# A nanmax over 65536 rows on one Trainium2 core: one tile's write-backs counted on their engines' own semaphores

## The chip, the cores and the metric

The kernel runs on one core of one Trainium2 chip. The metric is the device time of one execution in microseconds. Three engines do the arithmetic: VectorE (DVE in the profile), ScalarE (ACT) and GpSimd (POOL). SyncE (SP) only issues the DMA transfers. TensorE is not used.

## The reference

```python
def setup_inputs():
    batch, seq, dim = 32, 2048, 2048
    x = np.random.randn(batch, seq, dim).astype(np.float32)
    mask = np.random.rand(batch, seq, dim) < 0.1
    x[mask] = np.nan
    return {"x": x, "axis": -1}

def reference(x, axis):
    return np.nanmax(x, axis=axis).astype(np.float32)
```

For each of 65536 rows of 2048 floats, a tenth of them NaN, the largest value that is not NaN. The input is 537 MB; the output is 65536 floats.

## The kernel before, in words

**The work on one element.** VectorE's reduction with `max` needs the NaNs out of the way first, and that takes two passes over the upper 16 bits of each float, both in place in the tile. In the first, ScalarE makes a *key* (line 271, `kt<-xt`): it reads the upper halves of a tile `xt` and writes 16-bit keys into a key buffer `kt`. In the second, the *write-back*, the keys are turned back into upper halves in `xt`, with the NaNs now very low numbers. Most write-backs are done by GpSimd (line 281, `xt<-kt`), some small ones by ScalarE itself (line 271 too, `xt<-kt`). Then VectorE reduces whole rows to their maxima (line 288).

**Tiles.** A tile is 128 partitions by 28 quarters of a row (a quarter is 512 columns, so a full tile is 14336 columns, 7 rows in each partition). There are 74 tiles in 6 groups; three tile buffers, `xt0` to `xt2`, are used in turn, tile 64 being in `xt0`. Maxima of the first groups go to `acc`, those of tiles 61 to 74 to `lead`, which is how the profile tells them apart. The list `TILES` gives for each tile, in quarters: how it is loaded, in which pieces it is keyed and written back, and which maxima are taken. In the pieces a negative number is a piece that ScalarE writes back, a positive one a piece of GpSimd; a float (`-4.0`) tells that ScalarE's write-back is issued behind the next key. The tiles around the change are

```python
    + [([16, 12], [-4.0, 12, 12], [4, 12, 12])]     # tile 63
    + [([17, 11], [-4.0, 12, 12], [16, 12])]        # tile 64
    + [([17, 11], [11, 6, (4, -7)], [8, 8, 12])]    # tile 65
```

Tile 64 is loaded in 17 and 11 quarters. Its first 4 quarters (2048 columns) are ScalarE's, the next 12 (6144 columns) GpSimd's, and so are the last 12. Its first maximum takes 16 quarters, that is the first two pieces at once; its second takes the last piece. Tile 63 has the same pieces, but a maximum for each of them.

**Key buffers.** Three, `kt0` to `kt2`, of 6144 columns each, used in turn. A key that opens a buffer waits until those that read the buffer's last keys, the write-backs, are done: `kfree` holds these events. In addition, the last key of a tile waits for those who read the *next* buffer's keys (lines 410 to 412), so that the next tile's first key needs no wait for them. In tiles 63 and 64 alike the three pieces go to `kt0`, `kt1` and `kt2`.

**Order and waits.** The program is written out by hand; each engine works through its instructions in order. `Order.add` (line 166) gives each instruction the waits that it needs: an event is a semaphore and a count, waits that another wait already implies are dropped (`needed`, line 150), the last one is put on the instruction, and the others stand alone in front of it. Normally an instruction counts on its engine's own semaphore (`act`, `pool`, `dve`).

**Pairs.** An instruction can be given a semaphore of its own instead. Where one maximum needs one write-back of GpSimd and one of ScalarE, and no other maximum needs either, `joints` (line 91) makes the two a pair: both count on one semaphore, `pair64_1` in tile 64, and the maximum waits for its count 2. `cleaned` (line 369) then notes that one event, count 2, as the event of both write-backs, in `kfree` too.

**Loads.** SP issues the loads in order; a load waits until the last maximum of the tile that had the buffer is done. They all go through one queue.

Of the kernel before, what the change touches and what calls it, by code (L numbers as in the profile page):

```python
# [54 lines left out]
FLAGGED = (3, 5)  # L55
LATE = 4

APART = ()
WIDE = 7
BUFS = 3  # L60

# [29 lines left out]
def joints(pieces, reds):  # L91

    flat = []
    at = 0
    for step, parts in enumerate(pieces):  # L100
        for c in parts if isinstance(parts, tuple) else (parts,):

            if with_last(c):
                flat[-1] = (flat[-1][0], at + abs(c), False, step)
            else:
                flat.append((at, at + abs(c), c < 0, step + isinstance(c, float)))
            at += abs(c)
    needs = []
    done = 0
    for n in reds:  # L110
        over = [i for i, (a, b, _, _) in enumerate(flat) if a < done + n and b > done]
        done += n
        pools = [i for i in over if not flat[i][2]]
        backs = [i for i in over if flat[i][2]]
        if pools and backs and flat[pools[-1]][3] > flat[backs[-1]][3]:
            backs = []
        needs.append(pools[-1:] + backs[-1:])
    pairs = {}
    for need in needs:
        if len(need) == 2 and all(sum(i in n for n in needs) == 1 for i in need):  # L120
            for i in need:
                pairs[i] = tuple(need)
    return pairs
# [61 lines left out]
def kernel(  # L185
# [146 lines left out]
    for gi, (s, g) in enumerate(zip(rows, GROUPS)):  # L332
# [6 lines left out]
        for loads, pieces, reds in g:  # L339
# [19 lines left out]
            pairs = {}  # L359
            if number not in APART:  # L360
                pairs = joints(pieces, [n // Q for n in reds])
# [178 lines left out]
```

## Time and profile before

| | |
|---|---|
| median of three runs | 1254.84 us (1254.7 to 1254.85) |
| the profiled execution | 1254.63 us |
| its span, first to last instruction | 1253.3 us |
| read from HBM | 536.87 MB, 429 GB/s over the span |
| reductions to `acc`, 4 rows, 8192 columns | 53 of 8.687 us |
| reductions of 3 rows, 6144 columns | 6.544 us (`acc`), 6.546 us (`lead`) |
| GpSimd write-backs of 6144 columns | 64 of 7.041 us |
| ScalarE keys of 6144 columns | 64 of 5.321 us |

All times on the profile's axis are counted from the first instruction. Line 271 holds both of ScalarE's operations; `kt<-xt` is a key and `xt<-kt` a write-back. The timeline merges neighbouring instructions of a line, gives the first start, the time from there to the last end and the number of them, and in brackets how long the engine was idle before and what ended that. The chain of waits follows back from the last instruction what each step waited for.

### The profile page before, as it was taken

How to read it: one execution, taken by the hardware profiler on the slowest of the kernel's cores; microseconds unless marked ns; L12 is line 12 of the kernel's file. 1: busy time of each engine (PE TensorE's matmuls, PEld its weight loads, DVE VectorE, ACT ScalarE, POOL GpSimd, SP SyncE). 2: the span in 40 equal slices, each digit the busy share in tenths (PEclk: the TensorE clock that was granted, in tenths of full speed). 3: DMA queues.
4: the chain of work that ended last, by engine and by line, in shares of the span. 5: the costliest groups of instructions: out<-in, count | busy, mean ns of one | idle time of the engine just before them, and what ended most of it. 6: DMA issues, size and time to landing. Idle time of an engine off the chain costs nothing.

```text
span 1253.3 us, 892 instructions
## 1 busy us (share of the span) xinstructions
DVE 1111.0 (89%) x187; ACT 968.2 (77%) x281; POOL 1165.2 (93%) x240
## 2 busy tenths in 40 slices
DVE  0888989888889988898988888898888899899999
ACT  3777887778777877788777877776777779889997
POOL 2999989998999899998999899999999999899997
DMA  9999999999999999999999999999999999999996
GB/s 414 439 421 428 439 439 440 432 417 439 439 438 436 430 425 439 439 437 436 426 428 439 439 437 434 419 437 439 437 436 430 425 439 426 436 433 428 432 425 269
DMA packets 16855, 537.20 MB, mean 429 GB/s; under 512 B 2640, under 2 KB 2640, under 8 KB 4944
## 3 DMA queue, kind: packets, MB, share of 16 engines
q1 hardware_dynamic: 16848, 537.14, 99.2%
q14 instruction: 7, 0.06, 0.0%
HBM read 536.87 MB, written 0.26 MB: 429 GB/s over the span
## 4 chain that ended last, share of the span: by engine, by line
DMA 35%; DVE 34%; POOL 19%; ACT 10%; issue 0%; SPq 0%
DMA xt<-in_x_dram 35%; DVE acc L288 22%; POOL xt L281 19%; DVE lead L288 13%; ACT kt L271 9%; ACT xt L271 1%; SPq L247 0%; DVE none L294 0%; DVE lead L308 0%; SPq L265 0%; SPq L256 0%
## 5 line engine op out<-in xcount | busy, mean ns | idle before, releaser
L281 POOL TENSOR_SCALAR xt<-kt 128x6144 int16<-128x6144 uint16 (+10 forms) x234 | 1164.1, 4975 | 80.5 <-ACT kt L271 66.6
L271 ACT ACTIVATE kt<-xt 128x3584 uint16<-128x3584 int16 (+10 forms) x249 | 912.7, 3705 | 272.7 <-DMA xt<-in_x_dram 242.2
L288 DVE TENSOR_REDUCE acc<-xt 128x3 f32<-128x6144 f32 (+4 forms) x121 | 894.8, 7435 | 133.5 <-POOL xt L281 126.2
L288 DVE TENSOR_REDUCE lead<-xt 128x1 f32<-128x2048 f32 (+4 forms) x59 | 212.4, 3682 | 3.5 <-POOL xt L281 3.5
L271 ACT ACTIVATE xt<-kt 128x512 int16<-128x512 uint16 (+4 forms) x30 | 57.1, 1912 | 0.6
L271 ACT ACT_TABLE_LOAD x1 | 1.3, 1283 | 3.3 <-PEq L265 3.3
L314 DVE MEMSET lead<- 128x1 f32 x1 | 0.1, 59 | 3.3 <-PEq L265 3.3
L288 DVE TENSOR_REDUCE xt<-xt 128x1 f32<-128x1536 f32 (+1 forms) x2 | 2.4, 1211 | 0.0
L294 DVE TENSOR_SCALAR none<-acc 128x414 int32<-128x414 f32 x1 | 0.6, 593 | 0.0
L294 POOL TENSOR_SCALAR lead<-lead 128x91 int32<-128x91 f32 x1 | 0.5, 547 | 0.1
L308 DVE TENSOR_TENSOR acc<-acc,none 128x414 int32<-128x414 int32 x1 | 0.6, 586 | 0.0
L308 POOL TENSOR_TENSOR lead<-lead 128x91 int32<-128x91 int32 x1 | 0.4, 378 | 0.1
L521 POOL MEMSET const-float32-0.0<- 128x1 f32 x1 | 0.1, 99 | 0.2 <-issue 0.2
L271 ACT ACTIVATE lead<-lead 128x1 f32<-128x1 f32 x1 | 0.2, 203 | 0.0
L294 DVE TENSOR_SCALAR none<-lead 128x7 int32<-128x7 f32 x1 | 0.2, 169 | 0.0
L308 DVE TENSOR_TENSOR lead<-lead,none 128x7 int32<-128x7 int32 x1 | 0.2, 163 | 0.0
L521 POOL MEMSET const-bfloat16-1.0<- 128x1 bf16 x1 | 0.1, 103 | 0.0
L521 POOL MEMSET const-uint8-127<- 128x1 uint8 x1 | 0.1, 102 | 0.0
L521 POOL MEMSET const-float32-1.0<- 128x1 f32 x1 | 0.1, 99 | 0.0
## 6 DMA issues: line engine op xcount, KB each, us to landing
xt<-in_x_dram SPq DMA_DIRECT2D x61, 7168.0 KB, 22.6
xt<-in_x_dram SPq DMA_DIRECT2D x3, 4096.0 KB, 16.8
xt<-in_x_dram SPq DMA_DIRECT2D x5, 2048.0 KB, 23.7
xt<-in_x_dram SPq DMA_DIRECT2D x3, 3072.0 KB, 23.6
xt<-in_x_dram SPq DMA_DIRECT2D x2, 4352.0 KB, 16.3
xt<-in_x_dram SPq DMA_DIRECT2D x3, 2816.0 KB, 23.1
xt<-in_x_dram SPq DMA_DIRECT2D x2, 3584.0 KB, 21.3
xt<-in_x_dram SPq DMA_DIRECT2D x5, 1024.0 KB, 25.1
```

Source lines behind the costliest of these rows:

```text
L271: lambda: nc.scalar.activation(**kw),
L281: lambda: nc.gpsimd.tensor_scalar(**kw),
L288: return order.add("dve", nc.vector, lambda: do(**kw), deps)
L294: lambda: engine.tensor_scalar(out=none, in0=acc, scalar1=NONE, scalar2=float(0x00800000), op0=ALU.is_equal, op1=ALU.mult,),
L308: lambda: engine.tensor_tensor(out=bits, in0=bits, in1=none, op=op),
L314: e_warm = order.add("dve", nc.vector, lambda: nc.vector.memset(warm, 1.0), [])
L521: nc = _bacc.Bacc("TRN2", target_bir_lowering=False, num_devices=1)
```

## The change

Tile 64 is put on a list of tiles that have no pairs:

```diff
-APART = ()
+APART = (64,)
```

The list is read in one place, line 360: `if number not in APART: pairs = joints(...)`. In tile 64 the write-back of ScalarE then counts on `act` and that of GpSimd on `pool`. The waits that follow from it, as `Order` writes them (everything else is the same but for the numbers of the counts):

```diff
  # VectorE: the first maximum of tile 64, 16 quarters
-   waits pair64_1
+   waits act, pool
  # ScalarE: the last key of tile 64, kt2 <- xt0, 6144 columns
-   waits pool, load9, pair64_1
+   waits pool, load9, act
  # ScalarE: the second key of tile 65, kt1 <- xt1, 3072 columns
-   waits nothing
+   waits pool
```

No instruction is added, taken away or moved on any engine, apart from the wait in front of the maximum that stands alone.

## The prediction

> **What bounds the kernel now.** I read the page first: its shares, then section 4. The shares name no single bound.
>
> ```profile
> DVE 1111.0 (89%) x187; ACT 968.2 (77%) x281; POOL 1165.2 (93%) x240
> ...
> DMA 35%; DVE 34%; POOL 19%; ACT 10%; issue 0%; SPq 0%
> ```
>
> The load queue is busy for 99.2% of the span (section 3) and GpSimd for 93%, yet the chain changes hands, so I asked for it in order of time, from tile 64 on (1072 us to the end).
>
> ```profile
> 1079.80 5.33 ACT kt L271
> 1085.13 0.07 issue
> 1085.20 7.06 POOL xt L281
> 1092.26 0.02 issue
> 1092.28 6.55 DVE lead L288
> 1098.83 0.01 issue
> 1098.84 144.79 DVE lead L288 x45
> 1243.63 0.84 issue
> 1244.47 6.68 DVE lead L288 x3
> ```
>
> From 1092.28 on the end is set by VectorE reductions alone. Just before, three steps stand one after the other: GpSimd's write-back (1072.73 to 1079.76), then a ScalarE key, then GpSimd again. The waits from 1050 us to the end say the same: VectorE waits once in all that time.
>
> ```profile
> ACT kt L271 <- POOL xt L281: 9.2, 4, 4.9
> DVE lead L288 <- POOL xt L281: 3.5, 1, 3.5
> ACT kt L271 <- DMA xt<-in_x_dram: 1.4, 2, 0.9
> ```
>
> The longest wait in line 1 (4.9) is ScalarE's at 1079.80, and the 3.5 is VectorE's at 1092.28. The timeline shows both, and tile 63 beside them:
>
> ```profile
> 1057.52 2.48 ACT L271 ACTIVATE xt<-kt 128x2048 int16<-128x2048 uint16 x1
> 1060.03 5.32 ACT L271 ACTIVATE kt<-xt 128x6144 uint16<-128x6144 int16 x1
> ...
> 1072.39 2.47 ACT L271 ACTIVATE xt<-kt 128x2048 int16<-128x2048 uint16 x1
> ...
> 1079.80 10.11 ACT L271 ACTIVATE kt<-xt 128x6144 uint16<-128x6144 int16 x2 [4.94 <-POOL xt L281]
> ```
>
> In tile 63 ScalarE goes from its write-back to the tile's last key in 0.03 us (1057.52 + 2.48 = 1060.00, then 1060.03). In tile 64, with the same pieces, it stands still for 4.94 us.
>
> **Why it waits, and what the change does there.** The last key of a tile waits also for whoever last read the key buffer that comes next (lines 410 to 412). For tile 64 the key goes to kt2 and the next buffer is kt0, which ScalarE's own small write-back (2048 columns) read. But that write-back is half of a pair (lines 369 to 381): its entry is the pair's event, count 2, and the second count is GpSimd's write-back of the other 6144 columns, out of kt1. So ScalarE waits for GpSimd over a buffer that GpSimd does not use. Tile 63 has a maximum of its own for its small piece, hence no pair, hence no such wait. With tile 64 in APART the entry becomes ScalarE's own count. Both programs have the same instructions in the same order on each engine; the waits differ in three places.
>
> **1. The last key of tile 64.** It still has three waits, two of them standing alone as before. They are due: the load of its columns, issued 1050.37, landing 21.6 later, 1072.0; GpSimd's write-back of tile 63, that frees kt2, 1065.60 + 7.05 = 1072.65; ScalarE's write-back, 1072.39 + 2.47 = 1074.86. With tile 63's 0.03 the key starts at 1074.89, not 1079.80: 4.91 earlier. Ended at 1074.89 + 5.32 = 1080.21.
>
> **2. GpSimd behind it.** It follows a key by 0.08 (1085.12 to 1085.20), so its write-back runs 1080.29 to 1087.33 in place of 1085.20 to 1092.25.
>
> **3. VectorE.** Back to back, a reduction starts 0.08 before the recorded end of the last: two of 6.54 and 8.68 make 15.14 from 1073.65, ending 1088.79. The next can start at 1088.71 instead of 1092.28: 3.57. The one after it, at 1098.84, now 0.01 behind its forerunner, wins its 0.08 of overlap as well: 3.66 in all. Its data are there: the load issued 1065.11 lands 17.2 later at 1082.3, the key takes 4.88 (1087.2), GpSimd 1087.41 to 1093.89, wanted at 1095.18. The Trainium skill (VectorE: DVE Perf Modes, The DRAIN you can't avoid) says that the next operation does not start until the pipeline has emptied. By that rule nothing of the overlap is regained and the sum would be 3.49; the trace's 15.14 speaks for 3.66.
>
> **4. The maximum's two waits.** One more standing wait on VectorE, ScalarE's count, due at 1074.86, while the reduction in front runs to 1080.20; GpSimd's count, on the instruction, is due at 1079.76 as before. Behind it are tile 64's second maximum and the load that refills xt0. A gain is excluded, since a wait is only added. The floor is 0: the last maximum of the kernel has a standing wait too, done at 1243.63 in the chain, and it lies inside reductions that run on without a gap (1240.09 to 1246.76, 6.67 for three of 2.28). The ceiling is a lost overlap and a restart, 0.08 + 0.03. I take 0, by that row, which is the same engine and the same kind of wait. If ScalarE's write-back came after 1080.1, this wait would cost what it came late.
>
> **5. A key of tile 65** (kt1, 3072 columns) now waits for GpSimd's write-back out of kt1, which the pair had covered. That ended at 1079.76 and the key can't start before 1087.1: cover 7 us, cost 0.
>
> **What is late next.** SP issues each refill when a maximum frees the buffer, so these go 3.6 earlier, but the load engines have no idle time to win: their share is 1.00 from 1092 to 1190, and the last load lands at 1243.15 either way. So I held VectorE's starts, moved by 3.66, against the write-backs with loads kept where they are. Two narrow places:
> - The third write-back of tile 66. Its load lands at 1080.23 + 18.4 = 1098.64, ScalarE's write-back before the first key ends about 1098.9, and keys and write-backs of 3584, 4608 and 6144 columns (key 3.16, then GpSimd 4.19 and 5.35, the third GpSimd 7.06 behind a 5.32 key that waits for the first write-back) end at 1118.79. VectorE wants it at 1122.61 - 3.66 = 1118.95.
> - The last maximum:
>
> ```profile
> 1240.81 4.17 POOL L281 TENSOR_SCALAR xt<-kt 128x1536 int16<-128x1536 uint16 x3 [0.18 <-ACT kt L271]
> ...
> 1246.67 4.48 DVE L288 TENSOR_REDUCE lead<-xt 128x1 f32<-128x2048 f32 x2
> ```
>
> The last write-back, tied to the last loads, is ready at 1244.98 + 0.03 = 1245.02 (from the unrounded times); the last reduction starts at 1248.86. So 3.84 is the most that can come through, and 3.66 fits with 0.18 to spare.
>
> **The sum.** 3.66 off the profiled execution's 1254.63 (span 1253.3, 1.3 around it) is 1250.97. The median of the runs is 1254.84, 0.21 above it: 1251.2.
>
> **Rivals.**
> 1. *The loads take part of it back.* Nearly every margin behind 1092 shrinks to some tenths. If the loads of the last 161 us (1082 to 1243) came 0.6% later relative to VectorE, 1 us, about 0.8 would be lost after the 0.18: 1252.0. For it: the margins; against: landings follow one another steadily here. The Trainium skill (SBUF — State Buffer, A bandwidth-pool intuition that's wrong) holds that "HBM is almost always your end-to-end bottleneck, not SBUF". In its strict form, an end that hangs on the last load alone, nothing moves: 1254.8, since that load lands at 1243.15 either way. The 3.84 between its write-back and its maximum speaks against that form. Chances: 0.12 for a part, 0.02 for the strict form.
> 2. *The key waits for something else anyway*, so the change doesn't do what it says: if the GpSimd count that it still waits for were that of 1079.76, or its load landed late, nothing would move: 1254.8. Against: these two are due at 1072.65 and 1072.0. Chance 0.08.
> 3. *Slower: GpSimd stretches.* VectorE and GpSimd run side by side without pause; GpSimd is busy for 146 us after 1092. If its write-backs grew by 2.6%, 3.8 us, the gain would be gone; at 5%, 7.3 - 3.8 = 3.5 slower, 1258.3. Against: the 6144-column write-back takes 7.03 to 7.06 with ScalarE idle or busy. Chance 0.04.
>
> **How the numbers follow.** The forecast, the whole gain within some tenths (1250.9 to 1251.6), has 0.74. About 0.2% (2.5 us) is what a measurement of this kernel can tell from no change: below 1252.3 counts as faster. Rival 1 lies mostly there (0.11), so faster 0.85; same 0.01 + 0.02 + 0.08 = 0.11; slower 0.04. The range goes from 1250.8 (the 3.84 and the runs' spread of 0.15) to 1252.6, which takes in most of rival 1 and holds about 0.84.
>
> **What would show it.** The key at 1074.9, GpSimd at 1080.3, no wait of VectorE after 1050, reductions without a gap from 1048 to some 1247.5; last load still near 1243.1. A key still at 1079.8 proves rival 2; VectorE waits of tenths near 1119, 1134 or the end, rival 1; longer GpSimd rows of the same shape, rival 3.

## The result, and the profile after

Ten runs of the changed kernel give a median of 1251.48 us (1251.3 to 1251.79), ten of the kernel before 1254.86 (1254.42 to 1255.21). The ratio is 0.9973, 95% interval 0.9964 to 0.9983: 3.4 us faster. The prediction was 1251.2, range 1250.8 to 1252.6.

The page of the changed kernel, in the order of the lines shown of before (busy time of the engines; the chain's shares):

```profile
DVE 1111.1 (89%) x187; ACT 968.8 (77%) x281; POOL 1164.7 (93%) x240
...
DMA 38%; DVE 35%; POOL 16%; ACT 9%; issue 1%; SPq 1%
```

The shares hardly tell the two kernels apart. The waits from 1050 us to the end do (who waited for whom, total, times, longest):

```profile
POOL xt L281 <- ACT kt L271: 11.2, 16, 1.8
ACT kt L271 <- DMA xt<-in_x_dram: 10.1, 7, 4.1
ACT kt L271 <- POOL xt L281: 0.4, 1, 0.4
```

VectorE's 3.5 is gone, ScalarE's waits for GpSimd fell from 9.2 to 0.4, and ScalarE now waits for loads (1.4 before, 10.1 now). The timeline of ScalarE in tile 64:

```profile
1072.52 2.47 ACT L271 ACTIVATE xt<-kt 128x2048 int16<-128x2048 uint16 x1
1075.02 5.33 ACT L271 ACTIVATE kt<-xt 128x6144 uint16<-128x6144 int16 x1
1082.46 4.90 ACT L271 ACTIVATE kt<-xt 128x5632 uint16<-128x5632 int16 x1 [2.12 <-DMA xt<-in_x_dram]
```

The key follows the write-back by 0.03, as tile 63's does, and the next key waits for its load. The chain in order of time shows both what was won and what was not:

```profile
1067.33 7.71 DVE lead L288 x2
1075.05 5.12 issue
1080.17 106.07 DVE lead L288 x24
...
1197.68 28.08 DMA xt<-in_x_dram
...
1225.87 1.92 ACT kt L271
...
1227.86 2.49 POOL xt L281
...
1230.37 13.92 DVE lead L288 x7
```

The "issue" of 5.12 us, time in which the profile shows nothing that VectorE waited for, is no idle time. It begins where the maximum's standing wait, the one that the change adds, was done (1075.05), but at that moment the reduction in front was still running, until 1080.26. VectorE's own timeline shows one run of 51 reductions through this moment to the end, with no wait long enough to be listed:

```profile
1073.71 174.31 DVE L288 TENSOR_REDUCE lead<-xt 128x3 f32<-128x6144 f32 x51
```

What was not won stands at 1197.68: a load reaches into the end of the chain again. There are three gaps in the run, too short to be listed: the reductions at 1216.84, 1225.80 and 1230.37 start 0.02, 0.10 and 0.09 behind the recorded end of the one in front, where others start 0.08 ahead of it. That is 0.10 + 0.18 + 0.17 us lost.

The profiled executions of this document differ by up to 1.0 us before tile 64, whose first maximum starts between 1080.07 and 1081.07 in them. The clean measure of what the change touches is therefore the stretch from the start of tile 64's first maximum to VectorE's last end: 171.43 us before, 168.25 after, 3.18 less.

### The profile page after: what moved, and what is told of

Read it like the earlier page. It is cut to its first block, busy times and chain, and to the rows that moved or that the text cites. A ratio compares the mean times of both kernels' runs of the same rounds, so it can differ in the third digit from the quotient of the medians.

```text
span 1250.2 us, 893 instructions
## 1 busy us (share of the span) xinstructions
DVE 1111.1 (89%) x187; ACT 968.8 (77%) x281; POOL 1164.7 (93%) x240
## 4 chain that ended last, share of the span: by engine, by line
DMA 38%; DVE 35%; POOL 16%; ACT 9%; issue 1%; SPq 1%
DMA xt<-in_x_dram 38%; DVE acc L288 22%; POOL xt L281 16%; DVE lead L288 13%; ACT kt L271 8%; ACT xt L271 1%; SPq L247 1%; DVE xt L288 0%; DVE none L294 0%; DVE acc L308 0%; DVE lead L308 0%; SPq L265 0%; SPq L256 0%
```

## The experiments

**Theory:** ScalarE's last key of tile 64 no longer waits for GpSimd's write-back. **Rival:** the maximum's two waits, or the semaphores of their own, bring the gain. The first three experiments part them. A second question is where the tenths at the end went. The DMA rows hold a hint: one 8192-byte packet of the queue of instructions stands at 1211.4 in the changed kernel (rows by queue from 1210.5 to 1213), while before it stood at 1244.7 (1244 to 1246), behind the last load:

```profile
q1 hardware_dynamic: 142, 1.04, 99.8%
q14 instruction: 1, 0.01, 0.8%
```

```profile
q14 instruction: 1, 0.01, 1.7%
```

**e1: only the wait of the key taken away.** The pair stays. A tile on the list ALONE leaves out the wait of lines 410 to 412; tile 65's first key then waits for the pair itself, which is done by 1079.79, while that key starts at 1082.42.

```diff
-ALONE = (65,)
+ALONE = (64, 65)
```

> Tile 64 keeps its pair, its one semaphore and the single wait of its first maximum; only the last key of tile 64 no longer waits for the readers of the next key buffer (tile 64 joins tile 65 on the list ALONE), and tile 65's first key waits for the pair instead. Theory (the gain is ScalarE's last key of tile 64 freed from GpSimd's write-back): key at about 1074.8, VectorE without a wait after 1050, time 1251.0 to 1251.5. Rival (the gain comes from the way the maximum waits or counts): key as it was, 1254.9. A second question, the 0.5 us lost after 1216 in the changed kernel: if that comes from the instruction fetch (8192 bytes) that its one additional VectorE instruction moved from 1244.7 to 1211.4, among the last loads, then here, with VectorE's instructions as before, the fetch stands behind the last load again, which lands near 1243.1 and not 1243.8, and the time is at the lower end, about 1251.0 to 1251.2. If the loss belongs to VectorE being early, it appears here too: 1251.5.

Measured: 1251.11 (1250.9 to 1251.2); ratio to before 0.9969 (0.9958 to 0.9981). Key at 1074.76, the instruction packet at 1244.8, last load 1242.93. The chain, from 1072 on, is VectorE alone:

```profile
1067.23 176.42 DVE lead L288 x51
1243.65 1.49 issue
1245.14 2.29 DVE lead L288
```

The whole gain needs neither the list APART nor a second wait of the maximum; and without the additional VectorE instruction nothing is lost at the end: 167.75, 3.68 less than before. The rival is out. Repeated (e1_again) it gave 1251.05, and 167.75 again.

> The first experiment again, on the same chip as the one beside it, as its measure: 1251.0 to 1251.2.

**e2: only the wait put back.** The semaphores of the change, but the key waits for GpSimd's write-back out of kt1.

```diff
 kold = kold + last(kfree[(key + 1) % NKEYS])
+if number == 64:
+    kold = kold + last(kfree[(key + 2) % NKEYS])
```

> The changed kernel (two semaphores, two waits of the maximum), with the last key of tile 64 made to wait for GpSimd's write-back out of kt1 again, now through GpSimd's own count. Theory: key at 1079.8, VectorE's wait of 3.5 back at 1092.3, time 1254.9. Rival (semaphores of their own are what helps): 1251.5.

Measured: 1254.97 (1254.7 to 1255.59), ratio 1.0 (0.9991 to 1.0009). Waits from 1050 us on:

```profile
...
ACT kt L271 <- POOL xt L281: 9.3, 4, 4.9
DVE lead L288 <- POOL xt L281: 4.4, 2, 3.7
```

The 4.9 and VectorE's wait are back (3.7 at 1093.3; this execution reached tile 64 0.7 later, so the key stands at 1080.75). The counts of their own bring nothing by themselves.

**e3: the pair avoided in a third way.** The first maximum of tile 64 is split as in tile 63.

```diff
-    + [([17, 11], [-4.0, 12, 12], [16, 12])]
+    + [([17, 11], [-4.0, 12, 12], [4, 12, 12])]
```

> The kernel before, with the first maximum of tile 64 split as in tile 63 (4 and 12 quarters), so that no pair arises and APART stays empty. Theory: the key is freed as in the change, VectorE pays one more reduction start, 2.28 + 6.54 - 0.08 in place of 8.68, 0.06 us: 1251.3 to 1251.6 (the additional VectorE instruction moves the instruction fetch as in the change, so the last load lands near 1243.8). Rival (the list APART or the two waits do it): 1254.9.

Measured: 1251.49 (1251.4 to 1251.86), as the change. Key at 1074.91; instruction packet at 1211.4; the stretch 168.37; the same gaps at 1216.84, 1225.81 and 1230.38. The last load landed at 1243.34, not at the 1243.8 expected. It is the pair, and what its event is used for, that cost the 3.5 us.

**e4: one more standing wait in the kernel before.**

```diff
+if number == 64 and not part and done == 16 * Q:
+    nc.vector.wait_ge(order.sems["act"], order.count["act"])
 e = dve(
```

> The kernel before with one more standing wait on VectorE in front of tile 64's first maximum, for a count of ScalarE's that is long due. Price of the wait: theory 0.00 us (the maximum starts at 1080.1, 0.08 before the recorded end of the reduction in front); rival: a lost overlap and a restart, 0.08 to 0.12, then hidden behind VectorE's 3.5 us wait. Time 1254.9 by both. The instruction fetch: if VectorE's instruction count places it, the last one stands at about 1211 here, the last load lands about 0.6 later than before (1243.8 against 1243.15), and the time does not move since VectorE is 3.84 us behind the loads. If not, the fetch stays near 1244.7.

Measured: 1254.94 (1254.4 to 1256.26), ratio 1.0001 (0.9992 to 1.001). The first maximum starts 0.083 before the recorded end of the reduction in front, as without the wait (0.084): its price is 0.00. And the instruction packet stands at 1211.6, the last load lands at 1243.80: one VectorE instruction moves the fetch, and the loads behind it are late. Here that costs nothing, since VectorE is 3.84 behind them in the kernel before.

**e5: the change, with one VectorE instruction less elsewhere.** The small memset at the start goes to GpSimd.

```diff
-e_warm = order.add("dve", nc.vector, lambda: nc.vector.memset(warm, 1.0), [])
+e_warm = order.add("pool", nc.gpsimd, lambda: nc.gpsimd.memset(warm, 1.0), [])
```

> The changed kernel with its one small VectorE memset at the start (one column) moved to GpSimd, so that VectorE has as many instructions as before the change in spite of the additional wait. If VectorE's instruction count places the last instruction fetch: it goes back from 1211 to about 1241 to 1245, behind the last load, which lands near 1243.0; VectorE's gain of 3.62 us at 1100 stays whole to the end; time about 1251.1. If the fetch is tied to the two semaphores in tile 64, or if the loss at the end has another cause: fetch at 1211, last load near 1243.5, time 1251.5 as the changed kernel.

Measured: 1251.01 (1250.86 to 1252.05); ratio 0.997 (0.9959 to 0.9982). Packet at 1244.9, no gap, the stretch 167.75, as in e1, now with the two semaphores and the standing wait. So these cost nothing. The last load landed at 1243.45, later than expected, and did no harm; the loads that matter are those around 1216 to 1229.

**e6: the change, with lighter loads.** Half of the columns of tiles 72 and 73 are not loaded.

```diff
-e = load(xt[:, at : at + c], xg[:, base + at : base + at + c], before)
+d = c // 2 if number in (72, 73) else c
+e = load(xt[:, at : at + d], xg[:, base + at : base + at + d], before)
```

> The changed kernel, leaving out half of the columns of every load of tiles 72 and 73 (7.3 MB less, some 17 us of the load stream at 432 GB/s); all waits and all other instructions stay. Theory (the 0.5 us that the changed kernel loses after 1216 come from late loads): VectorE's lead of 3.62 us over the kernel before stays whole to the end, time about 1251.0 to 1251.2, with the instruction fetch still at about 1211. Rival (the fetch, or something else near 1211, holds up VectorE itself): the loss of 0.5 stays, 1251.5. A time far below, 1248 or less, would mean that VectorE does not set the end.

Measured: 1251.36 (1251.02 to 1251.94), between the two forecasts: the time does not decide it. The trace does, as far as one execution can. Its profiled execution came to tile 64 0.9 later than that of the change, but from there the stretch is 167.80, with the packet at 1212.3 and without the three gaps. So what is lost at the end in the change is lost by late loads; with the packet at this place VectorE itself is not held up.

**e7: eleven tiles on the list.**

```diff
-APART = (64,)
+APART = tuple(range(64, 75))
```

> All of tiles 64 to 74 on the list APART, so that 18 more maxima wait for two counts. Theory (a standing wait on VectorE that is due while the reduction in front runs costs nothing; the keys behind tile 64 are held by loads, not by GpSimd): 1251.1 to 1251.7, VectorE's reductions still in one run with an overlap of 0.08 each. Rival (each such wait breaks the overlap and costs 0.08 to 0.12): 1.4 to 2.2 more than the changed kernel, 1252.9 to 1253.7.

Measured: 1251.65 (1251.44 to 1252.26). VectorE now has 19 standing waits, where the change has 2 and e1 has 1 (17 more than the change, not the 18 of the expectation). It still runs through: 51 reductions in a row from 1074.27 take 173.93. The stretch is 167.87, 0.12 over e1's for 18 waits more, and the packet stands at 1221.2. The price by the rival was 1.4 or more over the change; the median is 0.17 over it, so that rival is out. The median is also 0.64 above that of e5, timed on the same chip. The profiled executions of the two differ by 0.51 ahead of tile 64 and by 0.12 behind it, so whether the 18 waits cost more than 0.12 in other executions stays open.

**e8: e1 with one more standing wait**, the lines of e4 added to e1.

> The first experiment (tile 64 on the list ALONE, its pair kept) with one more standing wait on VectorE, for a count long due. If the instruction fetch takes the 0.4 us: it moves from 1244.8 to about 1211, the last load lands 0.4 to 0.7 later, time 1251.5 in place of 1251.1. If the two counts on engines' own semaphores take it: 1251.1.

Measured: 1251.82 (1251.22 to 1252.21). Packet at 1211.6, gaps at 1225.98 and 1230.55, the stretch 168.20 against 167.75. The loss comes with one VectorE instruction more, with or without APART. The median is 0.3 above the forecast. The stretch accounts for 0.45 of the 0.7 over e1; the two were timed on different chips, on which the kernel before gave 1254.84 and 1254.75, and what is left is not explained.

**e9: e1 with less work for VectorE.** The second maximum of tile 64 leaves out half of the columns of each row.

```diff
-.rearrange("p (c d) -> p c d", c=m),
+.rearrange("p (c d) -> p c d", c=m)[
+    :, :, : D // 2 if number == 64 and m == 3 else None
+],
```

> The first experiment (tile 64 on the list ALONE), with tile 64's second maximum leaving out half of the columns of each of its three rows, so that VectorE has some 3.2 us less to do there. If VectorE's work alone still set the end: 3.2 less, 1247.9. If the loads stand right behind it, as the prediction's 3.84 us (last write-back ready against last maximum) says: only 3.84 - 3.72 = 0.1 to 0.2 us more than the first experiment comes through, 1250.9 to 1251.1, and VectorE's waits for GpSimd come back, some 3 us in all.

Measured: 1250.9 (1250.69 to 1251.27) against 1251.05 for e1 beside it. Waits from 1050 us on:

```profile
...
ACT kt L271 <- DMA xt<-in_x_dram: 9.8, 6, 3.9
DVE lead L288 <- POOL xt L281: 3.1, 3, 2.1
```

Of 3.2 us less work 0.15 came through by the medians, less than either kernel's runs spread; in the profiled execution nothing did, its stretch being 167.96 against e1's 167.75. The work saved came back as waits for write-backs. With the key freed, the loads stand right behind VectorE.

**The fetch, in the rows of one load.** The load of 1024 KB issued near 1197.6, before and in the change (size, us from issue to landing):

```profile
xt<-in_x_dram SPq DMA_DIRECT2D x1, 1024.0 KB, 27.6
```

```profile
xt<-in_x_dram SPq DMA_DIRECT2D x1, 1024.0 KB, 28.1
```

Its first part arrives at 1223.97 and 1224.02, its last but one of sixteen at 1225.11 and 1225.24, its last at 1225.12 and 1225.80: one part is some 0.6 late. The key that waits for it starts accordingly, before and in the change:

```profile
1225.19 4.23 ACT L271 ACTIVATE kt<-xt 128x2048 uint16<-128x2048 int16 x3 [0.25 <-issue]
```

```profile
1225.87 4.23 ACT L271 ACTIVATE kt<-xt 128x2048 uint16<-128x2048 int16 x3
```

The load in front of the first late one lands at 1210.95 before and at 1211.07 in the change, the first late one at 1213.39 and 1214.21. The time between these two landings tells whether the loads were held up here, however early or late the execution is. The stretch of each kernel, with the packet and this time:

| kernel | VectorE instructions against before | packet at | between the two landings, us | stretch, us | median, us |
|---|---|---|---|---|---|
| before | 0 | 1244.7 | 2.44 | 171.43 | 1254.86 |
| e4, one wait more | +1 | 1211.6 | 3.41 | 171.54 | 1254.94 |
| e2, wait put back | +1 | 1212.1 | 2.43 | 171.66 | 1254.97 |
| the change | +1 | 1211.4 | 3.14 | 168.25 | 1251.48 |
| e3, split | +1 | 1211.4 | 3.26 | 168.37 | 1251.49 |
| e8, e1 and one wait | +1 | 1211.6 | 2.95 | 168.20 | 1251.82 |
| e7, eleven tiles | +18 | 1221.2 | 2.41 | 167.87 | 1251.65 |
| e1, key freed | 0 | 1244.8 | 2.44 | 167.75 | 1251.11 |
| e5, change, memset moved | 0 | 1244.9 | 2.44 | 167.75 | 1251.01 |

The loads became late in four of the six kernels of the table that have the packet among them. In e2 it stands at the same place in the stream of loads, and in e7 ten us further on, and in these two executions no load behind it is late.

e1 and e5 beat both kernels, the change by 0.4 to 0.5 us.

## Why the prediction was right, and where it was off

- **The reason for the wait** (the pair's event standing for a buffer that GpSimd does not use): shown, by taking away that wait alone (e1), putting back that wait alone (e2) and avoiding the pair (e3).
- **Step 1, the key** at 1074.89: 1075.02, ScalarE's write-back ending 0.13 later in this execution; the 0.03 held. Rival 2 is out: the key no longer stood at 1079.8.
- **Step 2, GpSimd** at 1080.29: 1080.43.
- **Step 3, VectorE**, 3.57 and 3.66: counted from the first maximum of tile 64, the next reductions came 3.57 and 3.67 earlier. The second of these has the overlap that the prediction took the Trainium skill (VectorE: DVE Perf Modes, The DRAIN you can't avoid) to exclude. The same section adds that a next operation that is not held starts earlier, and this case's traces agree with that: 3.67 at that reduction and 3.68 over e1's whole stretch, not 3.49.
- **Step 4, the maximum's two waits**, 0: 0.00 in e4, no loss in e5, and 0.12 for 18 more of them in e7's profiled execution. What the step left out is that with one instruction more on VectorE an instruction fetch moves.
- **Step 5, tile 65's key**: it starts 0.09 before the recorded end of the key in front, at 1087.27. No wait.
- **Narrow places.** The third write-back of tile 66 was due at 1118.79 for a start at 1118.95; it ended at 1118.89 and VectorE started at 1118.99, without a gap. At the end 3.68 of 3.84 came through in e1, which leaves 0.16; e9's median is 0.15 lower and its stretch no shorter, so next to nothing is left.
- **The step that was off** is "loads kept where they are", with the last load at 1243.15 either way. It landed at 1243.82, and from the load at 1214.21 on they landed 0.7 to 0.8 later than before, of which 0.12 was there already. They became late just behind an instruction fetch that the change's one additional VectorE instruction had moved in among them. So of the 3.66 the profiled execution kept 3.18 (171.43 - 168.25), and the reductions, which the prediction had running without a gap, had three. That is rival 1 in part, with 0.48 lost where it reckoned with 0.8, and by a mechanism that it did not name. In its strict form (loads alone set the end) it is out.
- **Luck in the number.** The sum added 0.21 to get from the profiled execution to the median; for the change the two are equal, 1251.48. That made up for part of the 0.48, so that the median came out only 0.28 above the forecast.
- **Rival 3**, GpSimd stretching: its write-backs of 6144 columns took 7.05 at 1080.43 and 1111.84, beside VectorE without pause. Out.

## What to carry to other kernels

Where two producers share one count, every user of that event waits for the later of the two; look who else uses it, above all for buffers that only one of them touches. A single stall on a secondary engine is worth what the engine that sets the end is held up by it, and at most the slack of what stands behind: here 3.66 and 3.84, so almost all came through and nothing more will. When such a slack is down to tenths, even an instruction that costs its engine nothing can go with a loss of tenths, when it moves an instruction fetch in among the loads.

## What the runs showed of the hardware that was not expected

An 8192-byte instruction fetch is one packet of 0.31 us among those of the loads. With it at 1211.4 to 1211.6 (the change, e3, e4, e8) the next load landed 0.5 to 1.0 later behind the load in front of it than in the kernel before, so by more than the packet's own time, and the later ones stayed behind to the end. Where VectorE had no slack for it, the stretch was 168.20 to 168.37 against 167.75, 0.45 to 0.6 longer. That the fetch is the cause rests on its place just ahead of the first late load. It does not cost this each time: in e2 and e7 no load was late. Why not, and why it costs more than its 0.31 elsewhere, is open. The Trainium skill (Runtime: NRT & Kernel Launch, Instruction fetch mechanics) calls the cost of crossing a boundary between blocks of instructions mostly hidden; it was hidden in e2 and e7, and in e4, where VectorE had slack, and not in the change, e3 and e8.

Where the fetch stands goes with VectorE's last standing wait. In the five executions with as many VectorE instructions as before (before, e1, e1_again, e5, e9) it follows the end of that wait by 1.08 to 1.12 us. In the six with one more it stands 32 to 33 us ahead of that end, and in e7, with 18 more and a standing wait every few us, 25 ahead. That fits code of VectorE, fetched when its queue has passed a certain instruction, which one instruction more puts in front of the wait. No run moves that wait alone, so this is not shown.

A standing wait on VectorE is worked off while the reduction in front runs (done 1075.05, that reduction ending 1080.26), so that the chain of waits shows an "issue" of 5.12 us in which VectorE was busy throughout.

No run here leaves the NaNs in the tiles, so it is not shown that VectorE's maximum needs them out of the way.
